# A hybrid decoder trunk: w_out's additions on GpSimd, the norm's transposes between two products, a final norm in two parts

## The chip, the cores and the metric

The kernel runs on one core of one Trainium2 chip. The metric is the device time of one execution in microseconds (us); the median of three runs before the change is 2274.53 us (2274.50 to 2274.64).

A core has TensorE for matrix products (PE in the profile; PEld is its loading of weights), VectorE (DVE), ScalarE (ACT), GpSimd (POOL) and SyncE (SP), which here issues the DMAs. Each has a queue of its own and works through it in order. TensorE writes its products into PSUM banks; VectorE and ScalarE read them there.

## The reference

Two layers of a decoder trunk over 512 tokens of width 1024, in float32. Each layer norms its input, sends it through three branches (a state space scan, latent attention, a gated delta rule), mixes their outputs, and then does what this change is about:

```
h = x + mixed @ w_out                                             # 1024 x 1024
x = h + square(relu(rmsnorm(h, norm2_g) @ w_up)) @ w_down         # 1024 -> 4096 -> 1024
```

After the second layer comes a last norm, `rmsnorm(x, final_norm_g)`: each row of 1024 is divided by the root of its mean square and multiplied by a gain per column.

## The kernel before

**Exact products.** Every float32 operand of a large product is split in two: a rounded part (`hi`) and the rest (`lo`). `mm3` (L196) issues three products for each, hi x hi, hi x lo and lo x hi. A weight's split (`split_half`, L165) is a cast on ScalarE (L170, tile `whi`) and a subtraction on VectorE (L171, tile `wlo`); four buffers of each rotate.

**Seven products for eight.** `seven` (L1195) multiplies a 512 x 1024 operand with a 1024 x 1024 weight by a scheme of Strassen's kind: seven products of 256 x 512 by 512 x 512 instead of eight. They are named a11, a12, s1, s2, s3, s4 and a22, and each takes 24 instructions on TensorE (4 pieces of the depth, 2 token tiles, 3 for `mm3`). `h` has four row tiles of 128 tokens, each in two halves of 512 columns. Results gather in PSUM banks: a11, s2, s3 and a22 add up in the two banks `x`, s1 and s4 in two banks `z`, a12 has two small banks. After each product VectorE adds what stands in its banks to the part of `h` that it belongs to (L1219), so a bank must be read before the next product may write there. With `early`, the order is a11, a12, s1, s2, s4, s3, a22; rows 0 and 1 of `h` are then finished after s4, ahead of s3 and a22. Without it (the last w_down) the order is a11, a12, s2, s1, s3, s4, a22.

The scheme needs sums of weight blocks: p1 and p3 (`plus` in `seven_weights`, L1180), p2 (L1234) and p4 (`plus4`, L1247), eight additions of 128 x 1024 for a whole weight; and combinations of operand blocks, which w_out makes from the mixed branches in `comb` (L1297), 16 of 128 x 256, four each for s3, s1, s2 and s4. Those of s2 take s1's, and those of s4 take s2's. All are VectorE's before the change. `put` then splits a combination: a scaled copy on ScalarE (L1294) and a subtraction on VectorE (L1295).

**The norm behind w_out and w_down.** For each row tile the sum of squares is taken on ScalarE (`square`, L289), added up and scaled on VectorE (L293, L276) and raised to -1/2 on GpSimd (L277); VectorE multiplies the rows (L303). `norm_half` (L297) then transposes two row tiles on TensorE, 16 transposes of 128 x 128 in four groups of four, each group in one of three small banks (L308), and splits them on ScalarE and VectorE (L272, L273). The first half (rows 0 and 1) is emitted ahead of a22 by `before_last`; the second half stands inside the next stage.

**What sets the order.** A planner orders each engine's queue by priority, which is the order of the program, and by its own costs: an operation whose inputs it holds to be ready may pass others. `tc.high_priority()` lifts what is in its block. Where the planner's order is not wanted, `place` (L160) keeps a product under a key, and `behind` (L153) ties an instruction behind the product of a key; that is an order within TensorE's queue, without a wait. Before the change the first eight transposes of the first half are tied behind the first piece of a22.

**The end.** In the second layer `finish` (L1348) makes each row tile's scale with `row_scale`, multiplies both halves with scale and gain on VectorE (L1354) and stores each half by a DMA from SP's queue (L1355). Rows 0 and 1 are finished ahead of a22, rows 2 and 3 behind it, one after the other.

## Time and profile before

| What | Value |
|---|---|
| median of three runs | 2274.53 us |
| profiled execution, its own time | 2274.29 us |
| its span, first to last instruction | 2272.5 us |
| TensorE busy | 2252.4 us, 11758 instructions |
| VectorE busy | 1649.5 us, 3315 instructions |
| ScalarE busy | 1186.1 us, 2444 instructions |
| GpSimd busy | 65.0 us, 84 instructions |
| granted TensorE clock | 0.999 |

A row of a timeline has the start in us from the span's start, the duration in us, the engine, the line of the kernel, the operation, output<-inputs by the program's tile names, sizes, the number of merged instructions, and in brackets the engine's idle time before it and what ended that. A row of an answer on one line gives the shortest, median and longest duration in ns, and the first and last start. A row of the windows has the stretch and its length, then the busy time and the count of TensorE, its weight loads, VectorE, ScalarE and GpSimd, the granted clock, the DMA engines' share and GB/s. A matmul's shown duration is longer than its share of the pipe, as the next one starts before it ends.

The stretches that matter, in us from the span's start: w_out of the first layer up to 806.3, its second half from 744; the end of w_down of the first layer, 1104 to 1140; w_out of the second layer, up to 1933; the last w_down, 2225 to 2263.5, and the final norm behind it.

### The profile page before, as it was taken

The page shows a single profiled execution, that of the slowest core. Times are in us where ns is not written, and L with a number is a line of the kernel's source. Part 1 is how long each engine was busy: PE and PEld are TensorE (multiplying, and loading weights), DVE is VectorE, ACT ScalarE, POOL GpSimd, SP SyncE. Part 2 cuts the span into 40 slices and gives each one's busy share as a digit, 9 for nine tenths or more (in the row PEclk, how much of TensorE's full clock was granted, in tenths as well). Part 3 has the DMA queues.
Part 4 walks back from the last instruction along what each step waited for, and adds up shares of the span by engine and source line. Part 5 has one row for each costly group of instructions (what it writes and reads, how often), then busy time and mean ns, then how long its engine had stood idle before and what let it go on. Part 6 is the DMA issues. An engine that isn't in the chain of part 4 may idle for free.

```text
span 2272.5 us, 32127 instructions
## 1 busy us (share of the span) xinstructions
PE 2252.4 (99%) x11758; PEld 1867.6 (82%) x11758; DVE 1649.5 (73%) x3315; ACT 1186.1 (52%) x2444; POOL 65.0 (3%) x84
## 2 busy tenths in 40 slices
PE   9999999999999999999999999999999999999998
PEld 8888888888888888888888878888888887888886
DVE  7886567776766778767868865678657667778668
ACT  6666744333443555554656667443344435645545
POOL 1000000000000000000010000000001000000000
PEclk9999999999999999999999999999999999999999
DMA  4223633442225143233132246335422251433231
GB/s 143 81 75 110 190 108 119 137 134 75 84 65 176 56 149 111 93 110 103 52 99 81 71 121 195 104 110 148 121 84 75 66 189 34 167 112 102 84 111 47
DMA packets 220030, 244.07 MB, mean 107 GB/s; under 512 B 34256, under 2 KB 172384, under 8 KB 219872
## 3 DMA queue, kind: packets, MB, share of 16 engines
q1 hardware_dynamic: 219872, 242.02, 34.7%
q8 instruction: 92, 1.51, 0.3%
q14 instruction: 66, 0.54, 0.1%
HBM read 225.53 MB, written 11.74 MB: 104 GB/s over the span
## 4 chain that ended last, share of the span: by engine, by line
PE 95%; DVE 3%; DMA 1%; ACT 1%; issue 0%; POOL 0%; SPq 0%; DVEq 0%; POOLq 0%; ACTq 0%
PE acc L198 24%; PE acc L200 24%; PE acc L199 24%; PE sm L200 3%; PE sm L199 3%; PE sm L198 3%; PE sm L687 1%; PE sm L791 1%; DVE wlo L171 1%; PE yt L703 1%; PE sm L1073 1%; PE sm L802 1%; PE sm L1099 1%; PE yt L200 1%; PE yt L199 1%; PE yt L198 1%
## 5 line engine op out<-in xcount | busy, mean ns | idle before, releaser
L171 DVE TENSOR_TENSOR wlo<-wraw,whi 128x512 fp32r<-128x512 f32 (+1 forms) x536 | 365.4, 686 | 336.3 <-ACT whi L170 325.3
L170 ACT CAST whi<-wraw 128x512 fp32r<-128x512 f32 (+1 forms) x536 | 329.5, 618 | 524.1 <-PE acc L199 339.7
L198 PE MATMUL acc<-xh,whi 128*128 128x512 f32 (+1 forms) x1344 | 525.3, 391 | 0.0
L200 PE MATMUL acc<-xh,wlo 128*128 128x512 f32 (+1 forms) x1344 | 520.4, 388 | 0.0
L199 PE MATMUL acc<-xl,whi 128*128 128x512 f32 (+1 forms) x1344 | 519.2, 387 | 0.0
L200 PEld LDWEIGHTS acc<-xh,wlo 128*128 128x128 f32 x1344 | 252.5, 188 | 49.3
L198 PEld LDWEIGHTS acc<-xh,whi 128*128 128x128 f32 x1344 | 252.5, 188 | 48.4 <-ACT xh L272 0.4
L199 PEld LDWEIGHTS acc<-xl,whi 128*128 128x128 f32 x1344 | 252.7, 188 | 47.6 <-DVE xl L273 0.7
L170 ACT CAST whi<-wr 128x512 fp32r<-128x512 f32 x168 | 104.3, 621 | 107.9 <-PE acc L199 47.7
L198 PE MATMUL acc<-yh,whi 128*128 128x512 f32 x384 | 152.1, 400 | 0.0
L199 PE MATMUL acc<-yl,whi 128*128 128x512 f32 x384 | 150.3, 391 | 0.0
L200 PE MATMUL acc<-yh,wlo 128*128 128x512 f32 x384 | 149.8, 390 | 0.0
L171 DVE TENSOR_TENSOR wlo<-wr,whi 128x512 fp32r<-128x512 f32 x168 | 113.1, 685 | 35.6 <-ACT whi L170 34.7
L728 DVE SCALAR_TENSOR_TENSOR ckl<-acc,pc,ckl 128x511 f32<-128x511 f32 (+2 forms) x168 | 121.2, 743 | 19.2 <-ACT ckl L724 10.9
L198 PEld LDWEIGHTS acc<-yh,whi 128*128 128x128 f32 x384 | 71.5, 188 | 16.4 <-ACT yh L272 2.2
L200 PEld LDWEIGHTS acc<-yh,wlo 128*128 128x128 f32 x384 | 72.1, 188 | 15.1
L199 PEld LDWEIGHTS acc<-yl,whi 128*128 128x128 f32 x384 | 72.1, 188 | 14.2
L198 PE MATMUL acc<-whi,xh 128*128 128x512 f32 (+1 forms) x208 | 80.3, 386 | 1.2 <-DVE ckl L728 1.2
L199 PE MATMUL acc<-wlo,xh 128*128 128x512 f32 (+1 forms) x208 | 79.3, 381 | 0.0
L200 PE MATMUL acc<-whi,xl 128*128 128x512 f32 (+1 forms) x208 | 79.2, 382 | 0.0
L1219 DVE TENSOR_TENSOR h<-h,acc 128x512 f32<-128x512 f32 x120 | 76.9, 679 | 1.3 <-PE acc L200 1.3
L487 ACT ACTIVATE eE<-eE,cum 128x128 f32<-128x128 f32 x192 | 62.5, 390 | 27.9 <-DMA eE<-d_c 26.2
(468 smaller groups left out, 4497.8 us busy)
## 6 DMA issues: line engine op xcount, KB each, us to landing
wraw<-in_w_in_dram SPq DMA_DIRECT2D x144, 512.0 KB, 3.6
wraw<-in_w_up_dram SPq DMA_DIRECT2D x64, 512.0 KB, 3.5
wr<-in_w_down_dram SPq DMA_DIRECT2D x32, 1024.0 KB, 5.1
eE<-d_c SPq DMA_DIRECT2D x48, 256.0 KB, 4.1
wraw<-in_w_mla_out_dram SPq DMA_DIRECT2D x16, 512.0 KB, 3.4
eE<-d_e SPq DMA_DIRECT2D x32, 256.0 KB, 2.9
wraw<-in_w_ssd_out_dram SPq DMA_DIRECT2D x16, 512.0 KB, 3.3
wraw<-in_w_gdn_out_dram SPq DMA_DIRECT2D x16, 512.0 KB, 3.5
```

The source lines that it names most:

```text
L170: act.copy(hi, raw)
L171: dve.tensor_tensor(lo, raw, f32(hi), ALU.subtract)
L198: pe.matmul(o, ah, bh, start=start, stop=False, skip_group_check=more)
L199: pe.matmul(o, ah, bl, start=False, stop=False, skip_group_check=more)
L200: return pe.matmul(o, al, bh, start=False, stop=stop, skip_group_check=more)
L487: act.activation(o[:, i], o[:, i], AF.Relu, scale=-1.0, bias=cum[:, t, h0 + i : h0 + i + 1])
L687: pe.transpose(ps[:, n : n + P], pn[t][:, kb * P : (kb + 1) * P], ident)
L703: pe.matmul(o, v_h, th[:, c : c + w], start=kb == 0, stop=False)
L728: dve.scalar_tensor_tensor(acc[:, d:], ps[:, : S - d], taps_[3 - d], acc[:, d:], ALU.mult, ALU.add)
L791: x = pe.matmul(py[64 * i : 64 * i + 64, c * P : (c + 1) * P], xd[:, t, h * 64 : (h + 1) * 64], e2[h // 4][:, h % 4, :], start=True, stop= ...
L802: pe.matmul(po[:, c * P : (c + 1) * P], st[:, c * P : (c + 1) * P], ctl[:, tok], start=True, stop=True)
L1219: dve.tensor_tensor(hs_, hs_, ps[t], op)
```

## The change

1. In w_out (both layers) the eight additions of weight blocks and the 16 combinations go from VectorE to GpSimd (`adder=pool`; `comb` uses `pool`). w_down's stay on VectorE.
2. The transposes of the norm's first half are no longer tied behind a22's first piece. The scale and the multiplication of those rows get high priority. Where the order is `early`, the first products of s3 (the sixth product) are tied behind the last of s4 (the fifth). This holds for w_out in both layers and for the last part of w_down in the first layer.
3. In the last w_down, when one half of a row tile is settled (a12 settles the lower half of rows 0 and 1, s3 the upper half of rows 2 and 3), `settle` scales its part of the mean square (VectorE, 128 x 1) and multiplies this half by the gain in place (GpSimd, 128 x 512). `finish` then needs one VectorE operation ahead of the power, and multiplies the half that came last on VectorE by scale and gain, the settled one on ScalarE by the scale alone.

```diff
-    def mm3(o, ah, al, bh, bl, start, stop, more=False):
+    def mm3(o, ah, al, bh, bl, start, stop, more=False, key=None):
-        pe.matmul(o, ah, bh, start=start, stop=False, skip_group_check=more)
+        x = pe.matmul(o, ah, bh, start=start, stop=False, skip_group_check=more)
+        if key:
+            behind(key, x)
...
-    def norm_half(i, xs, ssq, gcol, pl, hs, ls, tag="xr", bufs=4, given=None, key=None):
+    def norm_half(i, xs, ssq, gcol, pl, hs, ls, tag="xr", bufs=4, given=None, first=False):
-            rs = row_scale(ssq[t])
-            xr.append(mk(pl, [P, D], F32, tag, bufs))
-            dve.tensor_scalar(xr[-1], xs[t], rs, None, ALU.mult)
+            with tc.high_priority() if first else nullcontext():
+                rs = row_scale(ssq[t])
+                xr.append(mk(pl, [P, D], F32, tag, bufs))
+                dve.tensor_scalar(xr[-1], xs[t], rs, None, ALU.mult)
...
-                x = pe.transpose(ps[:, j * P : (j + 1) * P], xr[j % 2][:, kk * P : (kk + 1) * P], ident)
-                if key and k < 4:
-                    behind(key, x)
+                pe.transpose(ps[:, j * P : (j + 1) * P], xr[j % 2][:, kk * P : (kk + 1) * P], ident)
...
-        def seven_weights(pl, w2d, r0):
+        def seven_weights(pl, w2d, r0, adder=dve):
-                    dve.tensor_tensor(o[:, q], x[:, q], y[:, q], ALU.add)
+                    adder.tensor_tensor(o[:, q], x[:, q], y[:, q], ALU.add)
...
                     if done and sq:
                         square(sq[r][:, j : j + 1], hs_, pl, "fs", 3 if nf == 4 else 2)
+                        if settled and i == j:
+                            settled(r, j)
...
-                place((tag, n, k, t), mm3(ps[t], ah, al, *w[k], start and k == 0, k == 3, not start))
+                key = (tag, "s4", 3, 1) if tag and early and n == "s3" and k == 0 else None
+                place((tag, n, k, t), mm3(ps[t], ah, al, *w[k], start and k == 0, k == 3, not start, key))
...
-                dve.tensor_tensor(o, p1[:, cs], b22[:, cs], ALU.add)
+                adder.tensor_tensor(o, p1[:, cs], b22[:, cs], ALU.add)
...
-                dve.tensor_tensor(p4[:, cs], halves[q], b21[:, cs], ALU.add)
+                adder.tensor_tensor(p4[:, cs], halves[q], b21[:, cs], ALU.add)
...
             def comb(x, y, op):
-                dve.tensor_tensor(s, x, y, op)
+                pool.tensor_tensor(s, x, y, op)
...
+        def settle(t, j, gb):
+            part_of[t] = mk(sp, [P, 1], F32, "npart", 4)
+            dve.tensor_scalar(part_of[t], h_ssq[t][:, j : j + 1], 1.0 / D, EPS, ALU.mult, ALU.add)
+            hs_ = h[:, t, j * 512 : (j + 1) * 512]
+            pool.tensor_tensor(hs_, hs_, gb[:, j * 512 : (j + 1) * 512], ALU.mult)
...
             if last:
-                rs = row_scale(h_ssq[t])
-                for i in range(2):
+                j = t // 2
+                rs = mk(sp, [P, 1], F32, "nrs", 4)
+                with tc.high_priority():
+                    dve.scalar_tensor_tensor(rs, h_ssq[t][:, 1 - j : 2 - j], 1.0 / D, part_of[t], ALU.mult, ALU.add)
+                    pool.tensor_tensor(rs, rs, nhalf[:, :1], ALU.pow)
+                for i in (1 - j, j):
                     hs_ = h[:, t, i * 512 : (i + 1) * 512]
-                    dve.scalar_tensor_tensor(hs_, hs_, rs, gb[:, i * 512 : (i + 1) * 512], ALU.mult, ALU.mult)
+                    if i == j:
+                        act.mul(hs_, hs_, rs)
+                    else:
+                        dve.scalar_tensor_tensor(hs_, hs_, rs, gb[:, i * 512 : (i + 1) * 512], ALU.mult, ALU.mult)
                     sync.dma_start(out[0][t * P : (t + 1) * P, i * 512 : (i + 1) * 512], hs_)
...
-                        norm_half(0, hts, h_ssq, lambda k: params[0][:, 124 + k : 125 + k], fp, *nx, "f", 4, key=((ly, "d"), "a22", 0, 0))
+                        norm_half(0, hts, h_ssq, lambda k: params[0][:, 124 + k : 125 + k], fp, *nx, "f", 4, first=True)
```

`n2` in w_out passes `first=not i` in the same way, and the last w_down passes `settled` to `seven`.

More of the change, by code (lines that the diff above doesn't have):

```diff
@@ L1193, in seven_weights, with seven @@
             return b, after
-        def seven(pl, ops, b, sq=None, before_last=None, fin=None, nf=4, pre=None, mid=None, prep=None, early=False, tag=None):
+        def seven(pl, ops, b, sq=None, before_last=None, fin=None, nf=4, pre=None, mid=None, prep=None, early=False, tag=None, adder=dve, settled=None):
             x, z = ([acc_bank() for _ in range(2)] for _ in range(2))
@@ L1277, in hybrid_kernel @@
             hts = [h[:, t] for t in range(T)]
-            b, after = seven_weights(wo, a["w_out"][ly], 0)
+            b, after = seven_weights(wo, a["w_out"][ly], 0, pool)
             for c in range(4):
@@ L1338, in n2 @@
                     nf.extend(hilo_tags(lp, "x"))
-                norm_half(i, hts, ssq, lambda k: col(g_n2 + k), pl, *nf, *tag, key=None if i else ((ly, "o"), "a22", 0, 0))
-            seven(wo, ops, b, ssq, lambda: n2(0, wo, "f", 2), nf=2, pre=forms, mid=mid, early=True, tag=(ly, "o"))
+                norm_half(i, hts, ssq, lambda k: col(g_n2 + k), pl, *nf, *tag, first=not i)
+            seven(wo, ops, b, ssq, lambda: n2(0, wo, "f", 2), nf=2, pre=forms, mid=mid, early=True, tag=(ly, "o"), adder=pool)
             xh, xl = nf
@@ L1346, in hybrid_kernel @@
             hd = mk(dr, [S, D], F32, "hd")
+        part_of = {}
+        def settle(t, j, gb):
[3 more added lines that the diff above has]
+            pool.tensor_tensor(hs_, hs_, gb[:, j * 512 : (j + 1) * 512], ALU.mult)
         def finish(t, gb):
             if last:
[L1351 to L1352 removed]
+                j = t // 2
[4 more added lines that the diff above has]
+                for i in (1 - j, j):
                     hs_ = h[:, t, i * 512 : (i + 1) * 512]
[L1354 removed]
+                    if i == j:
+                        act.mul(hs_, hs_, rs)
+                    else:
+                        dve.scalar_tensor_tensor(hs_, hs_, rs, gb[:, i * 512 : (i + 1) * 512], ALU.mult, ALU.mult)
                     sync.dma_start(out[0][t * P : (t + 1) * P, i * 512 : (i + 1) * 512], hs_)
@@ L1431, in before_last @@
                     if not last:
-                        norm_half(0, hts, h_ssq, lambda k: params[0][:, 124 + k : 125 + k], fp, *nx, "f", 4, key=((ly, "d"), "a22", 0, 0))
-                return dict(sq=h_ssq, before_last=before_last, fin=fin, prep=prep, early=not last, tag=(ly, "d"))
+                        norm_half(0, hts, h_ssq, lambda k: params[0][:, 124 + k : 125 + k], fp, *nx, "f", 4, first=True)
+                return dict(sq=h_ssq, before_last=before_last, fin=fin, prep=prep, early=not last, tag=(ly, "d"),
+                            settled=(lambda r, j: settle(r, j, gb[0])) if last else None)
             for qd in range(4):
```

## The prediction

> **What bounds the kernel.** I read the page first, then the chain of waits, then the timelines of TensorE, VectorE, ScalarE and GpSimd in the four places that the diff reaches.
>
> ```profile
> PE 2252.4 (99%) x11758; PEld 1867.6 (82%) x11758; DVE 1649.5 (73%) x3315; ACT 1186.1 (52%) x2444; POOL 65.0 (3%) x84
> PE 95%; DVE 3%; DMA 1%; ACT 1%; issue 0%; POOL 0%; SPq 0%; DVEq 0%; POOLq 0%; ACTq 0%
> ```
>
> TensorE is busy 99% of the span and the change removes no product, so only TensorE's gaps and the stretch behind its last product can be won. The timeline of TensorE in w_out of the first layer, from the first product of a12 to the first of w_up:
>
> ```profile
> 768.86 0.39 PE L198 MATMUL sm<-whi,xh 128*128 128x512 f32 x1
> ...
> 786.53 0.40 PE L200 MATMUL acc<-whi,xl 128*128 128x512 f32 x1
> 787.69 0.73 PE L198 MATMUL acc<-whi,s3h 128*128 128x512 f32 x2 [0.76 <-ACT whi L170]
> ...
> 797.20 0.39 PE L200 MATMUL acc<-whi,s3l 128*128 128x512 f32 x1
> 798.77 0.47 PE L198 MATMUL acc<-whi,ckh 128*128 128x512 f32 x1 [1.18 <-DVE h L1219]
> ...
> 799.53 1.47 PE L308 MATMUL sm<-ct,f 128*128 128x128 f32 x12
> 800.76 0.48 PE L198 MATMUL acc<-whi,ckh 128*128 128x512 f32 x1
> ...
> 806.27 0.28 PE L198 MATMUL acc<-xh,whi 128*128 128x256 f32 x1
> ```
>
> And the same gaps in the second layer, and at the end of w_down of the first layer, where 24 products of s3 run without a break:
>
> ```profile
> 1125.75 0.39 PE L198 MATMUL acc<-whi,mix 128*128 128x512 f32 x1
> ...
> 1130.97 0.39 PE L200 MATMUL acc<-whi,mix 128*128 128x512 f32 x1
> 1132.52 0.47 PE L198 MATMUL acc<-whi,yh 128*128 128x512 f32 x1 [1.17 <-DVE h L1219]
> ...
> 1914.34 0.74 PE L198 MATMUL acc<-whi,s3h 128*128 128x512 f32 x2 [0.76 <-ACT whi L170]
> ...
> 1925.41 0.47 PE L198 MATMUL acc<-whi,ckh 128*128 128x512 f32 x1 [1.18 <-DVE h L1219]
> ```
>
> One product takes (1130.97 - 1125.75) / 23 = 0.227 us. By that step the gaps are 787.69 - 786.53 - 0.23 = 0.93 us (gap 1), 798.77 - 797.20 - 0.23 = 1.34 us (gap 2), and 1132.52 - 1130.97 - 0.23 = 1.32 us at the layer's end. From 768.86 to 797.43 stand 120 products, 27.2 us of work in 28.6 us: gap 1 and 0.4 us in crumbs.
>
> **The combinations.** Why gap 1 is there, by VectorE's and ScalarE's timelines:
>
> ```profile
> 770.94 0.68 DVE L507 TENSOR_TENSOR mix<-mix,fs 128x512 f32<-128x512 f32 x1
> ...
> 783.28 0.42 DVE L1299 TENSOR_TENSOR fc<-mix,fc 128x256 f32<-128x256 f32 x1
> ...
> 785.50 1.27 DVE L1219 TENSOR_TENSOR h<-h,acc 128x512 f32<-128x512 f32 x2
> 786.69 0.68 DVE L171 TENSOR_TENSOR wlo<-wr,whi 128x512 fp32r<-128x512 f32 x1
> 787.29 0.41 DVE L1299 TENSOR_TENSOR fc<-mix,fc 128x256 f32<-128x256 f32 x1
> ```
> ```profile
> 787.74 0.42 ACT L1294 ACTIVATE xh<-fc 128x256 fp32r<-128x256 f32 x1
> ```
>
> The second combination of s4 stands on VectorE's queue behind the additions to h and a weight split; it comes at 787.29, its copy at 787.74 to 788.16, and only then can s4 go on. Two products of s3 were put in between, and these wait for a cast too. So s4 is late because of VectorE, not of the order alone. What VectorE carries there, and how long a GpSimd operation of the combinations' size takes:
>
> ```profile
> 769.00:797.50 28.50, 27.74 (x121) 21.86 (x119) 27.27 (x60) 19.45 (x42) 1.38 (x2) 1.00 0.00 1
> ```
> ```profile
> L519 POOL TENSOR_TENSOR yh<-yh,lrs x8: 608/625/1065, 34.2 to 1163.1; 128x256 f32<-128x256 f32 x8
> L1180 DVE TENSOR_TENSOR wp<-wr,wr x20: 1215/1217/1226, 722.1 to 2180.5; 128x1024 f32<-128x1024 f32 x20
> ```
>
> VectorE (the third busy number) is at 27.27 of 28.50 us. In that stretch 10 of the 16 combinations stand; back to back one takes some 0.34 us on VectorE (0.42, less the 0.08 by which neighbours overlap: two of 0.68 take 1.27 at 785.50), so 3.4 us leave it. On GpSimd they take 10 x 0.63 = 6.3 us, on an engine that is idle up to the norm. The last mixed rows arrive at 771.62 (770.94 + 0.68); a chain s1, s2, s4 of 10 operations is through by 778 to 782 (0.63 to 1.07 us each, median and longest of L519), ahead of 785.4, where s4's first six products begin (six steps before 786.76). Gap 1 would be gone: 0.93 plus 0.4 us.
>
> Against this stands what GpSimd does to VectorE while it reads SBUF:
>
> ```profile
> 1160.88 2.80 POOL L519 TENSOR_TENSOR yh<-yh,lrs 128x256 f32<-128x256 f32 x4
> ```
> ```profile
> 1161.47 1.15 DVE L171 TENSOR_TENSOR wlo<-wraw,whi 128x512 fp32r<-128x512 f32 x1
> ...
> 1164.84 0.68 DVE L171 TENSOR_TENSOR wlo<-wraw,whi 128x512 fp32r<-128x512 f32 x1
> ```
>
> The same split takes 1.15 us beside GpSimd and 0.68 us without: 0.47 us longer. If all 6.3 us were lost to VectorE, its stretch would be 27.27 - 3.4 + 6.3 = 30.2 us, 1.7 us more than the 28.5; if none, TensorE wins 1.3 us. The additions to h, one input of which is in PSUM, and VectorE's short waits take no harm from it, I suppose, so I take some two thirds of 6.3, 4.2 us: VectorE ends at 28.1, about full as now, but s4's operands are no longer the last thing on its queue. **0.5 us won per layer**, between +1.7 and -1.3.
>
> On this the Trainium skill, page "SBUF — State Buffer", section "SBUF: two separate sides", says that VectorE's operations with two SBUF inputs and GpSimd's share a port pair as an exclusive lock, held for a whole instruction. The trace agrees so far (0.47 us of a 0.63 us operation). By the rule in full, the stretch would be the 30.2 us worked out above, which is rival C.
>
> **The weight sums.** Eight per layer (four of L1180, two of L1234, two of L1247), 1.217 us each on VectorE. No row has a 128x1024 addition on GpSimd: at most 4 x 0.63 = 2.5 us, at least VectorE's 1.22; I take 2.2, nearer to the GpSimd row. The Trainium skill, page "GPSIMD Engine Reference", section "3.1 Elementwise — side-by-side cycle accounting", has 4.5 us for 2048 elements, by which an estimate for 1024 would be 2.25 us; no run here shows it. They start when the weights land (722 us). The six that make p1, p3 and p2 end by 722 + 6 x 2.2, or about 740 with waits; p1 is first split here:
>
> ```profile
> 771.54 0.68 DVE L171 TENSOR_TENSOR wlo<-wp,whi 128x512 fp32r<-128x512 f32 x1
> ```
>
> That is 30 us of cover. The splits that a 2.2 us addition can hold up there feed 12 products each (2.7 us), with four buffers: hidden, both ways, at **0**. If that cover were gone, one stall would be about 2.2 us. No DMA is added or moved; SP's queue changes only in what releases the output's DMAs.
>
> **The transposes.** Gap 2 is the bank's: s3's result must be added to h before a22 writes into the same bank. Today 12 transposes come after a22's first three products and take 800.76 - 799.53 = 1.23 us. Placed in the gap they cost nothing. For that the normed rows must be there when s3 ends:
>
> ```profile
> 795.42 1.38 POOL L277 TENSOR_TENSOR nrs<-nrs,nhalf 128x1 f32<-128x1 f32 x2 [101.70 <-DVE nrs L293]
> ```
> ```profile
> 797.28 0.75 DVE L303 TENSOR_SCALAR f<-h,nrs 128x1024 f32<-128x1024 f32 x1
> 797.94 1.28 DVE L1219 TENSOR_TENSOR h<-h,acc 128x512 f32<-128x512 f32 x2
> ```
>
> Today the second row is normed at 798.03, after s3's end, and it also holds up the addition to h by 0.3 us. With s3 wholly behind s4, s4 ends 24 products, 5.4 us, ahead of s3's end (now 22), and the priority lets the scale and the product pass a split (0.6 us): ready some 0.7 to 1.0 us before s3 ends. Where the rows are later than that, a22 waits behind the transposes on TensorE; even at today's 798.03 the 12 would end 0.5 us after the gap. The last four transposes need a fourth bank and stay inside a22. So 1.2 us at each of three places (both w_out, end of the first w_down): **3.6 us won**; at the least 0, where the planner does not use the gap.
>
> **The final norm.** From the timelines of the end (TensorE, VectorE, ScalarE, GpSimd, SP's issues, the DMAs):
>
> ```profile
> 2263.12 0.39 PE L200 MATMUL acc<-whi,yl 128*128 128x512 f32 x1
> ```
> ```profile
> 2262.19 2.07 DVE L1354 SCALAR_TENSOR_TENSOR h<-h,nrs,f 128x512 f32<-128x512 f32 x3
> 2264.18 0.68 DVE L1219 TENSOR_TENSOR h<-h,acc 128x512 f32<-128x512 f32 x1
> ...
> 2267.18 0.15 DVE L293 TENSOR_TENSOR nrs<-nss 128x1 f32<-128x1 f32 x1
> ...
> 2268.24 1.42 DVE L1354 SCALAR_TENSOR_TENSOR h<-h,nrs,f 128x512 f32<-128x512 f32 x2 [0.73 <-POOL nrs L277]
> ```
> ```profile
> 2265.49 0.19 ACT L289 ACTIVATION_READ_ACCUMULATOR fs<-h 128x1 f32 x1
> ```
> ```profile
> 2265.26 0.55 POOL L277 TENSOR_TENSOR nrs<-nrs,nhalf 128x1 f32<-128x1 f32 x1 [3.85 <-DVE nrs L276]
> ```
> ```profile
> L1355 SPq DMA_DIRECT2D out_dram<-h x8: 332/332/356, 2261.7 to 2269.7; - x8
> ```
>
> The products end at 2263.51, but row 3's addition waits until 2264.18 behind three of VectorE's final products, and its sum of squares, ready at 2265.68, waits until 2267.18 behind row 2's two. The change halves VectorE's share: one half of each row is multiplied by the gain ahead of time on GpSimd, and by the scale on ScalarE. Row 3 then: addition at 2263.55; squares 1.50 us after its start (2265.68 - 2264.18), 2265.05; one small operation for two, 0.3; power 0.55; both halves from 2265.93, ScalarE's taken to be no longer than VectorE's 0.75; the first stored from 2266.7, the second, one issue (332 ns) later, from 2267.0. Today the last issue starts at 2269.7. That is 2.7 us; ScalarE's product of row 2 may stand before row 3's square (0.3): **2.4 us won**, 1.4 if row 3's addition still queues.
>
> Its price is four 128x512 multiplications on GpSimd (1.2 us each, twice L519) and four scalar operations of 0.15 us, inside the last products. Two fall at 2238 to 2241:
>
> ```profile
> 2236.00:2247.00 11.00, 11.00 (x49) 8.93 (x48) 10.84 (x17) 6.62 (x13) 0.00 (x0) 1.00 0.14 44
> ```
>
> VectorE is at 10.84 of 11.00 us there, with the lower halves of s2's operands among it. Hidden: 0; in full: 2.4 us. I take **0.5 lost**, since TensorE has weight splits in hand there.
>
> **The sum** is -2 x 0.5 - 3.6 - 2.4 + 0.5 = -6.5 us. The profiled execution took 2274.29 us with its span of 2272.5; the median is 2274.53. So 2274.5 - 6.5 = **2268.0 us**. All at their good ends: -2.6 - 3.9 - 2.7 = -9.2, 2265.3.
>
> **Rivals.** B: the transposes don't land in the gaps (they need rows that the planner's costs may call late, or it cuts s3 open): -1.0 - 2.4 + 0.5 = -2.9, 2271.6. For it speaks that today's code had to tie them to a product by hand; against it, 0.7 us of room. D: VectorE keeps gap 1 in another form and the early gain costs its 2.4: -3.6 - 2.4 + 2.4 = -3.6, 2270.9. C, on the other side: the port. From the point where over 4.6 of the 6.3 us block VectorE, its splits, not ScalarE's casts, feed TensorE in s1, s2 and s4. Each w_out loses 1.7 us, its normed rows come late and gap 2 stays; the early gains cost 2.4; left are the tail and the end of w_down: 3.4 + 2.4 - 2.4 - 1.2 = +2.2, 2276.7. The 1.15 us split speaks for it; against it, that only a part of VectorE's operations read SBUF twice. E: the planner, given other costs, shuffles later stages, some us either way.
>
> **Chances.** Forecast 0.62, B 0.12, D 0.12, C 0.09, E 0.05. The range 2264.8 to 2272.6 holds the forecast with its ends, B and D. A change under 0.2% (4.5 us) is not told from none: faster (under 2270.0) takes nearly all of the forecast, and parts of D and E, 0.68; slower (over 2279.1) the bad ends of C and E, 0.07; the rest is 0.25.
>
> **What would show it.** Right: in TensorE's timeline the transposes directly behind s3's last product and a22 directly behind them, no wait of over 0.3 us before s4; the last output DMA issued within 3.9 us of the last product (now 6.2). Wrong: splits of w_out over 1 us long with TensorE waiting for them in s1 or s2 (C), transposes inside s3 or a22 and a wait of over 1 us before a22 (B), a wait before s2 or s1 of the last w_down (D).

## The result, and the profile after

The changed kernel takes 2289.95 us (median of 4 runs, 2286.81 to 2291.27) where the kernel before takes 2274.52 us beside it: a ratio of 1.0065 [1.0053, 1.0078], or 15.4 us more. 2268.0 was predicted, with a range of 2264.8 to 2272.6. The profiled execution took 2291.27 us with a span of 2289.3 us. Its page has for the busy time of the engines:

```profile
PE 2259.8 (99%) x11758; PEld 1872.2 (82%) x11758; DVE 1664.0 (73%) x3263; ACT 1186.5 (52%) x2448; POOL 143.0 (6%) x136
```

GpSimd carries 143.0 us in place of 65.0, and VectorE, though it has 52 instructions fewer (3263 against 3315), is busy 14.5 us longer. TensorE's waits of the changed kernel, largest groups first (us in all, times, longest):

```profile
PE acc L202 <- DVE wlo L171: 9.3, 3, 4.2
PE acc L201 <- DVE wlo L171: 5.3, 3, 1.9
```

Both are the lower half of a weight split, made by VectorE. None of them was in the kernel before. The windows view (TensorE, its weight loads, VectorE, ScalarE, GpSimd, granted clock, DMA share, GB/s) shows the place of the first, the stretch of w_out of layer 0 in which the weight sums are made; first the kernel before:

```profile
711.00:744.00 33.00, 33.00 (x147) 27.31 (x147) 24.39 (x40) 11.86 (x23) 0.00 (x0) 1.00 0.70 242
```

then the changed kernel:

```profile
711.00:744.00 33.00, 28.77 (x118) 23.31 (x117) 26.23 (x23) 10.21 (x22) 18.98 (x10) 0.90 0.70 237
```

TensorE gets 118 products done in place of 147, stands still for 4.2 us, and has a granted clock of 0.90. GpSimd's timeline in this stretch, then VectorE's, then TensorE's:

```profile
722.01 5.35 POOL L1181 TENSOR_TENSOR wp<-wr,wr 128x1024 f32<-128x1024 f32 x2 [0.28 <-ACT ckh L1298]
727.32 0.92 POOL L1303 TENSOR_TENSOR fc<-mix 128x256 f32<-128x256 f32 x1
728.20 5.09 POOL L1181 TENSOR_TENSOR wr<-wr,wr 128x1024 f32<-128x1024 f32 x2
733.25 5.29 POOL L1238 TENSOR_TENSOR f<-wp,wr 128x1024 f32<-128x1024 f32 x2
```
```profile
721.62 0.69 DVE L171 TENSOR_TENSOR wlo<-wraw,whi 128x512 fp32r<-128x512 f32 x1
722.23 2.88 DVE L508 TENSOR_TENSOR mix<-mix,h 128x512 f32<-128x512 f32 x1
725.03 2.61 DVE L1299 SCALAR_TENSOR_TENSOR ckl<-mix,ckh 128x256 fp32r<-128x256 f32 x1
727.56 0.96 DVE L1299 SCALAR_TENSOR_TENSOR s3l<-fc,s3h 128x256 fp32r<-128x256 f32 x1
728.44 2.62 DVE L1299 SCALAR_TENSOR_TENSOR ckl<-mix,ckh 128x256 fp32r<-128x256 f32 x1
730.99 2.58 DVE L1299 SCALAR_TENSOR_TENSOR s3l<-fc,s3h 128x256 fp32r<-128x256 f32 x1
733.50 6.80 DVE L171 TENSOR_TENSOR wlo<-wraw,whi 128x512 fp32r<-128x512 f32 x4
```
```profile
736.37 0.79 PE L202 MATMUL acc<-yh,wlo 128*128 128x512 f32 x1 [4.22 <-DVE wlo L171]
736.96 0.63 PE L198 MATMUL acc<-yh,whi 128*128 128x512 f32 x1
737.39 0.63 PE L201 MATMUL acc<-yl,whi 128*128 128x512 f32 x1
...
740.38 0.63 PE L202 MATMUL acc<-yh,wlo 128*128 128x512 f32 x1
```

These rows show a one-for-one alternation. Each VectorE operation with two SBUF inputs takes as long as the GpSimd addition beside it (2.58 to 2.88 us beside 5.35 / 2 = 2.7 and 5.09 / 2 = 2.5), whatever its own size; beside the small combination (0.92) it takes 0.96. VectorE has no idle time in these rows, so its splits do not wait for ScalarE's casts. Between the split at 721.62 and the next at 733.50 stand five such operations: 11.9 us where their own 0.69 (mixed rows, 128x512) and 4 x 0.42 us (operand halves, 128x256) would do, so the next weight split is some 9 us late, TensorE has used up the splits made ahead, and it waits for 4.22 us. After the wait its products go at a step of 737.39 - 736.96 = 0.43 us in place of 0.227, up to the one at 740.80: ten products in 4.4 us in place of 2.3.

The combinations do the same on a smaller scale. GpSimd, VectorE and TensorE of the changed kernel at the end of a12 and in s1 of layer 0, and at the end the window of the whole stage, the counterpart of the prediction's 769.00:797.50:

```profile
780.04 3.83 POOL L1303 TENSOR_TENSOR fc<-fc,mix 128x256 f32<-128x256 f32 x4
783.83 3.64 POOL L1303 TENSOR_TENSOR fc<-mix,fc 128x256 f32<-128x256 f32 x4
```
```profile
782.04 1.23 DVE L171 TENSOR_TENSOR wlo<-wp,whi 128x512 fp32r<-128x512 f32 x1
783.19 1.85 DVE L1299 SCALAR_TENSOR_TENSOR xl<-fc,xh 128x256 fp32r<-128x256 f32 x2
784.96 1.27 DVE L1220 TENSOR_TENSOR h<-h,sm 128x512 f32<-128x512 f32 x2
786.16 1.86 DVE L171 TENSOR_TENSOR wlo<-wp,whi 128x512 fp32r<-128x512 f32 x2
787.94 0.75 DVE L1299 SCALAR_TENSOR_TENSOR xl<-fc,xh 128x256 fp32r<-128x256 f32 x2
```
```profile
786.92 0.50 PE L201 MATMUL acc<-wlo,xh 128*128 128x512 f32 x1 [1.94 <-DVE wlo L171]
```
```profile
776.46:804.96 28.50, 26.47 (x116) 21.07 (x115) 26.94 (x48) 18.43 (x41) 10.64 (x12) 1.00 0.00 1
```

Two operand halves take 1.85 us beside GpSimd and 0.75 us after it, and a split 1.23 us; the additions to h, with one input in PSUM, keep their 1.27. In the middle of s1 TensorE waits 1.94 us for a split. Over the whole stage VectorE is not full: 26.94 of 28.50 us. Its delay is bunched at the stage's head.

The transposes stand where the prediction wanted them, directly behind s3's last product, with a22 directly behind them:

```profile
806.04 0.39 PE L202 MATMUL acc<-whi,s3l 128*128 128x512 f32 x1
806.27 1.56 PE L311 MATMUL sm<-ct,f 128*128 128x128 f32 x12
807.70 0.47 PE L198 MATMUL acc<-whi,ckh 128*128 128x512 f32 x1
```

And the end: TensorE's last product, and VectorE's rows from there.

```profile
2281.21 0.39 PE L202 MATMUL acc<-whi,yl 128*128 128x512 f32 x1
```
```profile
2281.92 0.75 DVE L1374 SCALAR_TENSOR_TENSOR h<-h,nrs,f 128x512 f32<-128x512 f32 x1 [0.73 <-POOL nrs L1368]
2282.59 0.68 DVE L1220 TENSOR_TENSOR h<-h,acc 128x512 f32<-128x512 f32 x1
...
2285.00 0.75 DVE L1374 SCALAR_TENSOR_TENSOR h<-h,nrs,f 128x512 f32<-128x512 f32 x1 [0.73 <-POOL nrs L1368]
```

From the start of the last product to the end of the span it is 2289.3 - 2281.21 = 8.1 us, before 2272.5 - 2263.12 = 9.4: 1.3 us shorter. Row 3's addition (2282.59) still stands behind row 2's final product (2281.92). The last output DMA is issued at 2286.2, 4.6 us after the last product's end (2281.60), where the prediction asked for at most 3.9.

**Where the time went.** The table has the starts of marked products in TensorE's timelines: for the kernel before in us, for each other profile how much later (+) than there. The columns behind "changed" belong to the runs below: "no sums" has the weight sums back on VectorE, "neither" the sums and the combinations, "transposes" and "norm" are these parts alone, "free" is the last run.

| mark | before | changed | no sums | neither | transposes | norm | free |
|---|---|---|---|---|---|---|---|
| first product of 352 columns | 10.73 | +0.34 | +0.15 | -0.08 | +0.17 | +0.32 | +0.44 |
| layer 0: a12 of w_out | 768.86 | +7.45 | +0.54 | -0.07 | +0.49 | +0.73 | +0.75 |
| first product of w_up | 806.27 | +7.79 | +0.84 | -0.60 | -0.06 | +0.70 | -0.18 |
| last s3 product of w_down | 1130.97 | +8.93 | +2.34 | +0.75 | +0.00 | +0.65 | +0.87 |
| layer 1: first product | 1139.89 | +8.10 | +1.48 | -0.09 | -0.81 | +0.66 | +0.03 |
| a12 of w_out | 1895.51 | +14.47 | +1.89 | +0.17 | -0.88 | +1.07 | +0.74 |
| first product of w_up | 1932.87 | +16.09 | +3.50 | -0.29 | -1.35 | +1.11 | -0.20 |
| s2 in the last w_down | 2236.01 | +16.11 | +3.57 | -0.22 | -1.35 | +1.11 | -0.27 |
| last product | 2263.12 | +18.09 | +5.59 | +1.74 | -1.37 | +3.08 | -0.29 |

In the changed kernel the weight sums cost 7.45 - 0.8 = 6.65 us in layer 0 (0.8 us of the lateness stands already ahead of the stage, where the change has no instruction: a group of four products, L1133 and L1132 before, starts at 697.89 in place of 697.10) and 14.47 - 8.34 = 6.13 us in layer 1 (8.34 at that entry). The last w_down loses 18.09 - 16.11 = 2.0 us, of which the tail gives 1.3 back. All marks of a kernel come from its one profile.

### The profile page after: what moved, and what is told of

It is laid out like the page before. It is cut to its first block, busy times and chain, and to the rows that moved or that the text cites. A ratio compares the mean times of both kernels' runs of the same rounds, so it can differ in the third digit from the quotient of the medians.

```text
span 2289.3 us, 32160 instructions
## 1 busy us (share of the span) xinstructions
PE 2259.8 (99%) x11758; PEld 1872.2 (82%) x11758; DVE 1664.0 (73%) x3263; ACT 1186.5 (52%) x2448; POOL 143.0 (6%) x136
## 5 line engine op out<-in xcount | busy, mean ns | idle before, releaser
L171 DVE TENSOR_TENSOR wlo<-wraw,whi 128x512 fp32r<-128x512 f32 (+1 forms) x536 | 375.3, 706 | 336.0 <-ACT whi L170 325.2
```

The costliest lines, as they stand in the source:

```text
L171: dve.tensor_tensor(lo, raw, f32(hi), ALU.subtract)
```

## The experiments

**Undoing the parts on GpSimd.** Three kernels. In the first the weight sums go back to VectorE, in the second the combinations, in the third both, so that transposes and final norm are left.

The first edit is in the first and third, the second in the second and third.

```
-            b, after = seven_weights(wo, a["w_out"][ly], 0, pool)
+            b, after = seven_weights(wo, a["w_out"][ly], 0)
...
-            seven(wo, ops, b, ssq, lambda: n2(0, wo, "f", 2), nf=2, pre=forms, mid=mid, early=True, tag=(ly, "o"), adder=pool)
+            seven(wo, ops, b, ssq, lambda: n2(0, wo, "f", 2), nf=2, pre=forms, mid=mid, early=True, tag=(ly, "o"))
```
```
-                pool.tensor_tensor(s, x, y, op)
+                dve.tensor_tensor(s, x, y, op)
```

> The weight sums of w_out go back to VectorE; the combinations stay on GpSimd, transposes and final norm as in the changed kernel. Theory L (GpSimd's lock): beside a GpSimd addition of 2.6 us each VectorE operation with two SBUF inputs gets one turn per addition, which starved TensorE for 4.2 us and then cost some 2 us more through a lower granted clock; from the entry of w_out to the first product of a12 the changed kernel lost 6.65 us (layer 0: 776.31 - 768.86, less 0.8 at the start) and 6.13 us (layer 1: 1909.98 - 1895.51 - 8.34). Without the sums on GpSimd these 12.8 us come back: 2277 us, no wait of over 1 us in the first product of w_out, granted clock 1.00 there; the 1.9 us wait in s2/s1 beside the combinations stays. Theory K (the combinations cost as much or more, the clock loss is theirs): over 2283 us.

Measured: 2278.19 us, ratio 1.0012 [1.0003, 1.0021] to 2274.98 us before. The 4.2 us waits are gone in both layers; in the stretch of the sums TensorE is busy throughout, at full clock:

```profile
711.00:744.00 33.00, 33.00 (x147) 27.35 (x146) 24.05 (x36) 11.95 (x24) 4.63 (x5) 1.00 0.69 240
```

The changed kernel stands 15.4 us over the kernel before, this one 3.2: the weight sums cost 12.2 us, near the 12.8 read off the marks. Theory L's forecast came, K falls.

> The combinations of w_out go back to VectorE; the weight sums stay on GpSimd. Theory L: the 4.2 us waits stay in both layers; only the 1.9 us wait per layer goes, and gap 1 (0.9 us) comes back: 2288 us, between 2285 and 2290. Theory K: 2279 us or less.

Measured: 2289.54 us, ratio 1.0064 [1.0050, 1.0078]. The waits for the split are 5.86 and 3.56 us. With the sums on GpSimd it makes 0.9 us of difference (15.4 against 14.6 us over the kernel before) where the combinations are.

> Weight sums and combinations both on VectorE, as in the kernel before; the transposes between the last two products and the final norm in two parts stay. By the prediction's steps: 2274.5 - 3.6 - 2.4 + 0.5 = 2269.0. By the trace of the changed kernel, in which the last products end 2.0 us later beside the gain on GpSimd and the tail is only 1.3 us shorter: 2274.5 - 3.6 + 0.7 = 2271.6. Theory K or a loss from the transposes themselves: above 2274.

Measured: 2274.94 us, ratio 1.0001 [0.9992, 1.0009]. Against the first run, 3.2 us come back: that is the price of the combinations on GpSimd, which the prediction had as a gain of 1.0. By the marks it is unevenly spread: w_out of layer 0 takes 0.8 us less here than in the first run, that of layer 1 takes 2.1 less, and of these some 1.6 are slow products, which followed the 1.93 us wait in layer 1 alone. And with nothing on GpSimd but the final norm's gain, the change wins nothing: the marks show w_out 0.5 us shorter in each layer (-0.07 to -0.60 in layer 0, +0.17 to -0.29 in layer 1) and the end of the first w_down 0.8 us, but 1.3 us lost in between, and 2.0 us at the last w_down.

**Is it the length of one GpSimd instruction, or its work in all, or VectorE's order?** The changed kernel, with each 128x1024 sum in four parts (p1 and p3 by the lines below, p2's halves and p4 likewise). VectorE's, ScalarE's and TensorE's instructions stand in the same order as in the changed kernel, from the first to the last.

```
-                for q in (slice(0, 1024), slice(1024, 2048)):
+                for q in [slice(i, i + st) for st in [256 if adder is pool else 1024] for i in range(0, 2048, st)]:
                     adder.tensor_tensor(o[:, q], x[:, q], y[:, q], ALU.add)
```

> The changed kernel with each 128x1024 weight sum on GpSimd cut into four of 128x256; VectorE's and TensorE's instructions stand in the same order, and GpSimd adds up as many elements. Theory L (a VectorE operation waits for one whole GpSimd instruction): a split beside the sums takes some 1.3 us in place of 2.6, below the 2.7 us that TensorE needs for its 12 products, so the 4.2 us waits go and with them the lower clock: 2277 to 2280 us. Rival O (it is the order on VectorE, in which the rows' mixes and operand halves stand ahead of the splits, or GpSimd's total time, not the length of one instruction): the wait stays at about 4 us and the time at 2290.

Measured: 2279.09 us, ratio 1.0017 [1.0009, 1.0026]. GpSimd is busy longer (160.2 us in all, against 143.0), and yet 11.3 us of the 15.4 are gone. GpSimd's and VectorE's rows, and the window of the stage:

```profile
721.92 6.72 POOL L1181 TENSOR_TENSOR wp<-wr,wr 128x256 f32<-128x256 f32 x8 [0.33 <-ACT ckh L1298]
...
729.30 8.03 POOL L1181 TENSOR_TENSOR wr<-wr,wr 128x256 f32<-128x256 f32 x8
```
```profile
730.33 4.58 DVE L171 TENSOR_TENSOR wlo<-wraw,whi 128x512 fp32r<-128x512 f32 x4
```
```profile
711.00:744.00 33.00, 33.00 (x147) 27.36 (x146) 22.32 (x29) 11.54 (x24) 24.39 (x28) 1.00 0.70 239
```

A split takes 4.58 / 4 = 1.15 us beside additions of 0.84 to 1.0 us on the mean, and TensorE does not wait in this stage, although VectorE stands still for 3.87 us (725.9 to 729.8) behind ScalarE's copy of a combination. So it is the length of the single GpSimd instruction that VectorE waits for; rival O falls. The delay is mutual: a quarter takes 0.73 us where VectorE does nothing (726.51 to 728.63), and 1.18 us beside its splits (732.03 to 735.50). On this the Trainium skill, page "SBUF — State Buffer", section "SBUF: two separate sides", has it that the two engines' port pair is an exclusive lock, held for the whole instruction: the 2.6 us operations of VectorE beside 2.6 us sums, and the 1.15 us ones beside quarters, agree.

**What lowers the clock after a wait?** The kernel before, in which ScalarE makes TensorE wait at the start of w_out.

```
                     w.append(split_half(raw(k)))
+                    if n == "a11" and k == 0 and tag and tag[1] == "o":
+                        for _ in range((24, 20)[tag[0]]):
+                            with tc.high_priority():
+                                act.copy(w[0][0], raw(k))
```

> The kernel before, in which ScalarE casts the first weight tile of w_out again, 24 times in layer 0 and 20 times in layer 1 (the same values into the same tile), so that TensorE has to wait at the start of w_out; GpSimd has no work there. From ScalarE's rows (0.54 us a cast back to back, from about 733.5; the products start at 741.65) the waits come to some 5.5 us in layer 0 and 3.3 us in layer 1. Theory W (the wait itself lowers TensorE's granted clock afterwards): 8 to 11 products at a step of 0.43 us in place of 0.227 follow each wait, some 2 us on top of it each time. Rival G (the clock falls because of GpSimd's work or of its lock): the products after the waits go at 0.227 us, and nothing comes on top.

Measured: 2298.05 us, one run, beside 2274.8. The waits came out longer than worked out, 9.89 and 7.29 us: a repeated cast takes 0.65 us (14 of them 9.05) in place of 0.54, and the casts of the next tiles stand among them. TensorE's timeline behind the first, and the window around it:

```profile
752.52 0.80 PE L198 MATMUL acc<-whi,ckh 128*128 128x512 f32 x1 [9.89 <-ACT whi L1211]
753.11 0.63 PE L199 MATMUL acc<-wlo,ckh 128*128 128x512 f32 x1
...
757.38 0.63 PE L200 MATMUL acc<-whi,ckl 128*128 128x512 f32 x1
```
```profile
735.00:765.00 30.00, 20.11 (x78) 16.15 (x77) 14.49 (x23) 20.58 (x36) 0.00 (x0) 0.83 0.24 82
```

Eleven products at a step of 0.43 us follow, and ten in layer 1, with GpSimd at 0.00. The marks agree: a12 is later still than the end of the wait, by 2.6 and 2.5 us (10.87 to 13.51 in layer 0, 21.09 to 23.63 in layer 1), which is eleven or ten steps of 0.2 and the slower first one. Rival G falls: GpSimd does nothing here. Theory W's forecast came: the slow products follow the wait, whoever causes it.

**The two other parts alone.** Sums and combinations on VectorE in both. In the first the final norm is as in the kernel before, so that only s3's place and the transposes are changed:

```
-                            settled=(lambda r, j: settle(r, j, gb[0])) if last else None)
+                            settled=None)
...
-                j = t // 2
...
+                rs = row_scale(h_ssq[t])
+                for i in range(2):
+                    hs_ = h[:, t, i * 512 : (i + 1) * 512]
+                    dve.scalar_tensor_tensor(hs_, hs_, rs, gb[:, i * 512 : (i + 1) * 512], ALU.mult, ALU.mult)
...
```

> Of the change, only s3 wholly behind s4 and the transposes between s3 and a22; weight sums, combinations and final norm as before. The prediction's step: -3.6, 2271.4 us. Theory T, from the marks of the run with transposes and norm together: the gap behind s3 is filled (0.5, 0.8 and 0.5 us won in net at the three places), but s4, which now has no product of s3 ahead of it, waits 1.31 us for its first operand in place of 0.93, and at the start of w_up of layer 0 VectorE waits 1.1 us longer for a weight transfer of w_down: -0.3 up to the last w_up and nothing behind it, 2274.7 us. If the late transfer is due to the final norm's part, it is gone here: 2273.3.

Measured: 2273.25 us, ratio 0.9994 [0.9985, 1.0003] to 2274.63, or 1.4 us less where the prediction had 3.6. The interval alone does not tell this from no change; the marks have -1.37 at the last product, in steps at the three places. TensorE ahead of s4 and behind s3:

```profile
788.71 0.50 PE L198 MATMUL acc<-whi,xh 128*128 128x512 f32 x1 [1.29 <-ACT xh L1298]
...
798.15 0.39 PE L202 MATMUL acc<-whi,s3l 128*128 128x512 f32 x1
798.38 1.61 PE L311 MATMUL sm<-ct,f 128*128 128x128 f32 x12
799.87 0.47 PE L198 MATMUL acc<-whi,ckh 128*128 128x512 f32 x1
```

The gap behind s3 is filled, but the wait ahead of s4 grew from 0.76 to 1.29 us, since the two products of s3 that stood there are behind s4 now. That is 0.5 us net per w_out (+0.49 to -0.06 and -0.88 to -1.35 in the marks). The late weight transfer is not in this run, so the time came out below the 2274.7 expected of theory T; it is not in the run with the norm alone either. See below.

In the second the final norm is the changed one, and the order is as before:

```
-                key = (tag, "s4", 3, 1) if tag and early and n == "s3" and k == 0 else None
+                key = (tag, "s4", 3, 1) if False else None
...
+                if key and k < 4:
+                    behind(key, x)
...
-                norm_half(i, hts, ssq, lambda k: col(g_n2 + k), pl, *nf, *tag, first=not i)
+                norm_half(i, hts, ssq, lambda k: col(g_n2 + k), pl, *nf, *tag, key=None if i else ((ly, "o"), "a22", 0, 0))
```

> Of the change, only the final norm in two parts. The prediction's step: -2.4 + 0.5 = -1.9, 2273.1 us. Theory N, from the same marks: the last products end 2.0 us later, since VectorE's operand halves and weight splits wait for the 1.7 us multiplications on GpSimd (1.78 us in place of 0.69), and the stretch behind them is 1.2 us shorter: +0.7, 2275.7 us. No wait for a transfer at w_up of layer 0; PE's last product 2.0 us later than before, against its own start.

Measured: 2276.21 us, ratio 1.0007 [0.9998, 1.0016], or 1.6 us more, which the interval alone does not tell from no change. The marks have 3.08 - 1.11 = 2.0 us lost in the last w_down, and the tail is 9.4 - (2274.3 - 2266.20) = 1.3 us shorter: theory N. The rest of the 1.6 us lies in stages that this part doesn't touch. The four prices as measured, 12.2 + 3.2 - 1.4 + 1.6 = 15.6 us, make up the 15.4 of the whole change. GpSimd's first pair of multiplications, and VectorE's rows beside it:

```profile
2239.71 3.22 POOL L1361 TENSOR_TENSOR h<-h,f 128x512 f32<-128x512 f32 x2 [301.36 <-DMA f<-in_final_norm_g_dram]
```
```profile
2240.00 1.78 DVE L271 TENSOR_TENSOR mix<-fs,mix 128x512 fp32r<-128x512 f32 x1
2241.71 1.77 DVE L271 TENSOR_TENSOR fx<-fs,fx 128x512 fp32r<-128x512 f32 x1
```

Each operand half waits for one multiplication (3.22 / 2 = 1.6 us) and takes 1.1 us more than the 0.69 of other such operations. TensorE waits 0.93 us for the first of them, in s2, and 0.31 us in s1 for a split that stands behind.

**Towards a version that beats both.** First, on top of the run with the transposes alone, the wait ahead of s4:

```
-                    with tc.high_priority() if d > 1 and n in ("a12", "s1") else nullcontext():
+                    with tc.high_priority() if (d > 1 and n in ("a12", "s1")) or (d < 2 and n == "s4") else nullcontext():
```

> As the run with the transposes alone, and the first two combinations of s4 get priority on VectorE, so that they stand ahead of the additions to h. Theory T: the wait of 1.3 us ahead of s4 goes in both layers: 2.6 us less than the transposes alone, 2272.1 us. Rival: a weight split or the addition to h takes the place of the wait (it is VectorE's whole load, 27 of 28.5 us, that counts): the same time as the transposes alone, within 0.7 us.

Measured: 2273.4 us, ratio 0.9996 [0.9987, 1.0004]: nothing won over the transposes alone. TensorE now waits 1.23 us for the lower half of the same operand instead of 1.29 for its copy. The rival's forecast came: to move one operation forward only puts another in its place. That VectorE's whole load sets this gap fits this, but was not tested further.

Next, the final norm without GpSimd: only rows 2 and 3 are multiplied by the gain ahead, on VectorE, rows 0 and 1 are finished as in the kernel before, and row 2's last products are put behind row 3's addition (VectorE's) and row 3's square (ScalarE's). The priority of the last run stays in.

```
-                        if settled and i == j:
+                        if settled and i == j and i == 1:
...
-            pool.tensor_tensor(hs_, hs_, gb[:, j * 512 : (j + 1) * 512], ALU.mult)
+            dve.tensor_tensor(hs_, hs_, gb[:, j * 512 : (j + 1) * 512], ALU.mult)
...
-            if last:
+            if last and t < 2:
+                rs = row_scale(h_ssq[t])
...
+            elif last:
...
+                    if t == 2:
+                        behind(("row 3", i == j), x)
```

> As the run with s4's combinations first, and a final norm in two parts of another kind: only rows 2 and 3 are multiplied by the gain ahead, on VectorE, in a stretch in which it waits for casts (0.7 us at a time between 2250 and 2258 in the kernel before); row 2's last products stand behind row 3's addition and square. By theory N: no operation waits for GpSimd, so the last product is 0.0 to 0.5 us later; the tail is some 2.1 us shorter: 2270.3 us. Rival: the settling on VectorE costs its 1.4 us in full: 2271.5. Rival: the order at the end doesn't count: 2272.1.

Measured: 2272.5 us, ratio 0.9990 [0.9981, 0.9999]. VectorE's rows of the settling, and of the end:

```profile
2253.50 0.68 DVE L1362 TENSOR_TENSOR h<-h,f 128x512 f32<-128x512 f32 x1
...
2263.33 0.68 DVE L1220 TENSOR_TENSOR h<-h,acc 128x512 f32<-128x512 f32 x1
2263.93 0.74 DVE L1383 SCALAR_TENSOR_TENSOR h<-h,nrs,f 128x512 f32<-128x512 f32 x1
```

The last w_down keeps its length (-0.97 at s2, -0.93 at the last product), so the settling costs nothing here, and the tail is 2270.0 - 2262.19 = 7.8 us, 1.6 less than before. The 2.1 us worked out were too many, since row 1's last product still holds row 3's addition for 0.7 us.

The same without that priority, and with one more tie in the branch of rows 0 and 1:

```
+                    if t == 1 and i == 1:
+                        behind(("row 3", False), x)
```

> As the run with the other final norm, but without the priority of s4's combinations, and with row 1's last product behind row 3's addition to h too. If VectorE's queue at the end sets the time: row 3's addition comes at once behind the last product, 0.6 us earlier than with that run, and the time is 2271.5 to 2272 us. Rival: row 1's and row 2's products, now both behind row 3's addition, hold up row 3's small operation, and nothing is won: 2272.5 us.

Measured: 2272.93 us, ratio 0.9993 [0.9984, 1.0002]. The tail is 2270.6 - 2263.04 = 7.6 us, 0.2 less (and the kernel is not told apart from that run by its time); the two products that now stand behind row 3's addition hold its small operation back to 2265.41. Mostly the rival's case.

And the other final norm without the priority and without the tie of s3 to s4:

```
-                key = (tag, "s4", 3, 1) if tag and early and n == "s3" and k == 0 else None
+                key = (tag, "s4", 3, 1) if False else None
```

> As the run with the other final norm, without the priority of s4's combinations, and without the tie of s3 behind s4: as in the kernel before, two products of s3 stand ahead of s4's operands; the transposes stand where the planner's costs put them, which here is behind a22's first product. Theory T: the wait ahead of s4 falls from 1.3 to 0.93 us, but the gap behind s3 comes back (1.3 us) and the transposes cost their 1.2 us again at two of three places: 2 to 3 us slower than with the tie, 2274.5 us. Rival: the tie does nothing, 2272.5 us.

Measured: 2271.68 us, ratio 0.9987 [0.9978, 0.9996], 3.1 us less than before and the lowest of all medians. Theory T falls here: TensorE's timeline has both the short wait ahead of s4 and the filled gap.

```profile
788.39 0.73 PE L198 MATMUL acc<-whi,s3h 128*128 128x512 f32 x2 [0.76 <-ACT whi L170]
...
797.96 0.39 PE L202 MATMUL acc<-whi,s3l 128*128 128x512 f32 x1
798.19 0.27 PE L311 MATMUL sm<-ct,f 128*128 128x128 f32 x1
798.84 1.42 PE L311 MATMUL sm<-ct,f 128*128 128x128 f32 x11 [0.38 <-DVE f L306]
800.02 0.48 PE L198 MATMUL acc<-whi,ckh 128*128 128x512 f32 x1
```

The expectation had the transposes behind a22's first product; twelve of them stand ahead of it. Each of the three places wins 0.8 to 0.9 us (+0.75 to -0.18, +0.87 to +0.03, +0.74 to -0.20). So it was enough to take the transposes' tie to a22 away and to give the normed rows priority; by the marks, the tie of s3 behind s4 cost 0.4 us in each w_out (0.55 and 0.47 won there with it, in the run with the transposes alone, 0.93 and 0.94 without).

## Why the prediction was wrong, step by step

**The weight sums** are the step that failed: "That is 30 us of cover", and of the splits, "hidden, both ways". They measured +12.2 us. The 30 us were counted for the sums' results, and these were in time. What was not counted is VectorE's queue: five operations with two SBUF inputs stand between two weight splits there, each but the one beside the small combination waits for a whole sum, and the splits made ahead, which carry TensorE for some 10 us (722.3 to 732.1), are used up before the next split comes. The prediction let one sum hold up one split; and its price without cover, "one stall would be about 2.2 us", was 4.22 and 4.21 us with 2.3 and 1.7 us more in slow products. The sum itself takes 2.40 to 2.86 us (single ones of L1181, L1238 and L1251), over the 2.2 taken; all but two are over the bound of 2.5. The estimate of 2.25 us from the Trainium skill, page "GPSIMD Engine Reference", section "3.1 Elementwise — side-by-side cycle accounting", is exceeded too. Part of this is VectorE's turns in between: the two sums of 2.40 us start beside additions to h that read PSUM, those of 2.8 us and more stand beside 128x512 operations with two SBUF inputs.

**The combinations**: 1.0 us won was forecast, 3.2 us were lost. The ten combinations took 9.3 us on GpSimd and not 6.3, but VectorE lost only 3.9 us to them in layer 0 (seven operations by 0.54 each, and one by 0.13), close to the "two thirds of 6.3, 4.2 us". What failed is the step from that total to "0.5 us won": VectorE ended with room (26.94 of 28.50 us busy, where 28.1 was worked out), but the loss falls between 779 and 788, ahead of a split that s1 needs, and a stage's total doesn't show that. That VectorE would be relieved at the stage's end, and gap 1 be gone, was right: s4 goes on without a wait in the changed kernel. The wait only moved to a split in s1, 1.94 and 1.93 us. That 3.2 lies near the bad bound (1.7 per layer) is luck: by the marks it is 0.8 and 2.1, and some 1.6 of the latter are the slow products behind one of the two waits, for which the prediction has no term.

**The transposes**: the mechanism was right, and the trace shows it as the prediction said. The size was off: 1.4 us in place of 3.6. Of the 1.2 us at each w_out, 0.5 goes to s4, which lost the two products of s3 ahead of it; that price of the edit "s3 wholly behind s4" was not in the sum. The rest of the difference is that the twelve transposes take 799.87 - 798.38 = 1.49 us and the gap had 1.34. At the end of w_down the normed row is 0.38 us late, which leaves 0.8.

**The final norm**: 2.4 us were forecast for the tail, 1.3 came; it is the case given with it, "1.4 if row 3's addition still queues". The settling's price was put at 0.5 and is 2.0, near its "in full: 2.4"; the reason given, that TensorE has splits in hand, is the same miscount as with the sums, since the two operand halves of s2 stand in the queue where the multiplications run. A multiplication takes 1.5 to 1.8 us, where 1.2 was taken.

**The rivals**: C, the port, was the mechanism, and its sign came: splits of 1.23 us in s1, with TensorE waiting 1.94 us for one. At 2276.7 it had only the combinations and the gain in it (3.4 + 2.4); for these two the runs have 3.2 + 2.0, of which the first agrees by luck, as said above: C was to begin where over 4.6 us block VectorE, and 3.9 did it. It left the sums out, 12.2 us of the 15.4: C had been weighed for an instruction of 0.63 us, in which a split loses 0.47, and not for one of 2.6. B did not happen. What D names came in part: VectorE's delay took another form, and the early gain cost 2.0 of its 2.4, with a wait of 1.38 us inside s1 of the last w_down, where D's sign was a wait before it. A gap ahead of s4 appears as soon as the combinations are back on VectorE.

## What to carry to other kernels

Before work is moved to GpSimd, list the two-SBUF-input operations in VectorE's queue while it runs, and charge each with one whole GpSimd instruction; it is the length of the single instruction that counts, so if it must go there, it goes in short pieces. Cover has to be counted for every queue that the moved work can hold up, not for the moved result alone, and at the place in the queue where the delay falls, not over the whole stage. And a wait of TensorE of some 4 us and more cost 1.7 to 2.6 us on top of it here.

## What the runs showed of the hardware that was not expected

TensorE's clock falls after a wait. The six waits of 3.56 to 9.89 us (two each in the changed kernel, the run with the combinations on VectorE and the run with the casts) were all followed by 7 to 11 products at a step of 0.43 us in place of 0.227. After 1.93 us it happened in three of the six waits of that length (the changed kernel, the first run and the run in quarters have two each, and one of the two was followed by 7 or 8 slow products), and began 1.0 to 1.9 us after the wait's end; after waits of up to 1.38 us it did not happen. It cost 1.6 to 2.6 us each time. It may be why the kernels with 1.93 us waits spread by over 4 us from run to run (2286.81 to 2291.27, 2276.05 to 2280.55, 2277.75 to 2281.89): in the run in quarters the longest execution has a mean granted clock of 0.996, the shortest 0.999. That is not shown, as each kernel has one profile.

The Trainium skill, page "TensorE: Matmul & The Clock Gate", section "Part 1: The HAM clock gate (the "warmup" mystery)", has the clock go to half after an idle window of some 3.4 us, and come back after as long a window of work, the windows running freely. The step of 0.43 us against 0.227 agrees with about half the clock. All six long waits are longer than such a window, though with windows that run freely only the 7.29 and 9.89 us are sure to hold a whole one; the slow stretch of 736.37 to 740.80 is 4.4 us. The three short waits don't agree: 1.93 us is less than a window. Two of the three slow stretches behind them last 3.41 us (1922.07 to 1925.48 in the changed kernel, 1909.03 to 1912.44 in the first run), as long as one window; that a window which is idle in part is enough would fit, but no run here tests it. The prediction has no term for the clock, since it had no wait of that length in it.

Left open is a wait of 0.9 to 1.1 us at the start of w_up of layer 0. VectorE's queue stands there behind a weight sum of w_down whose transfer lands some 2 us later than in the kernel before (in the run with both on VectorE, the sum starts at 820.00 in place of 818.19). It appears in the changed kernel, in the first and third run and in the last one (0.88 to 1.12 us), and is not there with the transposes alone or the norm alone; between the transposes alone and the run with s4's combinations first (0.6 us), which differ in w_out only, it came. What slows the transfer was not found.
